# Sparse attention's row maxima without their bf16 split, a third set of split weights, the output norm's products in PSUM, and the FFN's block sums spread over the first units

## The chip, the cores and the metric

One core of one Trainium2 chip runs the whole program. The metric is the time of one execution on the device in microseconds; lower is better. Every part of the program is issued from one TileContext with `schedule_with_timeline_sim=True`: the tile scheduler, not the text, fixes the order of each engine's instructions, and each engine then runs its own list in that order, waiting on semaphores.

## The reference

One layer over 1024 tokens of width 1024: three mixers on one normalised input, merged by gates, and a gated MLP behind them. Cut to what the change touches:

```python
sc = q . kc * scale - slopes * dist_c                 # compressed branch: softmax over 63 blocks
p_cmp = masked_softmax(sc, dist_c >= 0)               # also gives the importance for top-8 selection
o_sel = masked_softmax(q . k_sel[idx] ...) @ v_sel     # selected blocks
o_win = masked_softmax(q . k_win ...) @ v_win          # window of 512
out = g0 * o_cmp + g1 * o_sel + g2 * o_win
...
mixed = gm0 * (y_ssm @ w_br_ssm) + gm1 * (y_sb @ w_br_sb) + gm2 * (y_nsa @ w_br_nsa)
x = x + rms_norm(mixed @ w_out, post_mix_norm)
h = rms_norm(x, pre_ffn_norm)
u = causal_dwconv(h @ ffn_w_up)                       # 3 taps
gate, val = split(u)
f = (gelu(gate) * val) @ ffn_w_down                   # D_FF = 2816
x = x + rms_norm(f, post_ffn_norm)
```

## The kernel before

Activations lie transposed, channels on the 128 partitions and tokens along the row, in two halves `h` of 512 tokens. Nearly every large product is made of 128x512 matmuls into a PSUM bank called `dense` (five banks) by `mm` at L203. For accuracy each fp32 operand is split into `hi` (rounded by ScalarE) and `lo` (the rest, by a subtraction), and three matmuls hi·hi, lo·hi, hi·lo stand for one product. `load_w` (L262) loads a weight block of 128x1024 (`wraw`), rounds it on ACT (L267) and subtracts on POOL (L268); it has two sets of `whi`, `wlo`, so a third unit's splits wait until PE has done with the first. A unit of one half has 24 matmuls.

**Sparse attention** runs on 16 query blocks (two groups `g`, eight blocks `i`). `compressed` (L724) makes the compressed softmax in an SBUF tile `p` and the rows that are added to the query tile `Q1`; `maxima` (L803) has PE make the scores of a block once to find each row's maximum (reduces at L826), turns the maxima into a bf16 pair (L831 to L837, five small instructions, two of POOL's memsets beside them), transposes the four 32-column pieces and copies them into `Q1[96:128]` (L842), so that the score matmuls subtract the maximum themselves. `attend` (L844) makes the scores again, exponentials and values; `merge` (L884) transposes the result, divides and adds it to `yacc` (L889 to L893). These are generators; a driver takes steps of them in turn and fills the gaps with matmuls of the merge gates' weights (`dense<-h_hi`, `h_lo`).

**Output projection and first up-units.** For each half, eight units of `wo` are followed by two norms (`rstd`, L1336 to L1340: Ln, Exp and a Newton step) and products with the norm's row (L1353, L1354, L1360); each norm's sum comes from one matmul `psn<-osq`. The result is split into `h2[h, k]`. N_FIRST = 4 pairs of up-units (`up_half`) then run plainly, all of the first half of the tokens and then all of the second, and hide the norms. The sixteen squares of `h2` are then combined (`combos`, L1428 to L1431) and split (L1500, L1501, L1506, L1507) for the other 18 pairs, which use a seven-product block scheme (`weights7`, whose weight sums are POOL's: L1391 to L1405). `conv` writes the taps of a unit (L301, L305, L309); a gate's tile then takes its Gelu (L1442) and is multiplied and stored to `m_d` (L1445, L1446).

**Down projection.** `m_chunk` loads `m_d` in chunks (L1513), splits each tile on ACT (L1519) and DVE, and `down` multiplies it with `wdn` weights of four blocks. The first chunk is asked for inside the last up-pair. The residual input `x1` (two loads of 2048 KB, L1572) is loaded early in this stage.

Of the kernel before, what the change touches and what calls it, by code (L numbers as in the profile page):

```python
# [14 lines left out]
OP = mybir.AluOpType  # L15
# [25 lines left out]
def consts():  # L41
# [24 lines left out]
    aug[0, 32:34] = 1.0  # L66
    aug[1, 34:36] = 1.0
# [127 lines left out]
def trunk(ctx: ExitStack, tc: tile.TileContext, A: dict, outT: bass.AP, dbg=None):  # L195
# [66 lines left out]
    def load_w(src, n, tiles=None, raw=None):  # L262
        if raw is None:
            raw = wp.tile([128, n], F32, name="wraw", bufs=2)
        nc.sync.dma_start(raw, src)
        hi, lo = tiles or (wp.tile([128, n], R32, name="whi", bufs=2), wp.tile([128, n], R32, name="wlo", bufs=2))
        act(hi, raw, AF.Copy)  # L267
        (V if tiles else P).tensor_tensor(lo, raw, fl(hi), op=OP.subtract)  # L268
        return hi, lo
# [28 lines left out]
    def conv(o, h, ps, taps, bias, halo, by_act=False):  # L298

        n = len(taps) - 1  # L300
        act(o, ps, AF.Identity, bias=bias, scale=taps[0])  # L301
        if h == 1 and by_act:
            for d in range(1, n + 1):
                for t in range(d):
                    act(o[:, t:t + 1], halo[:, n - d + t:n - d + t + 1], AF.Identity, bias=o[:, t:t + 1], scale=taps[d])  # L305
        if h == 0:
            V.tensor_copy(halo[:, :n], ps[:, 512 - n:])
        for d in range(1, n + 1):
            V.scalar_tensor_tensor(o[:, d:], ps[:, :512 - d], taps[d], o[:, d:], op0=OP.mult, op1=OP.add)  # L309
# [250 lines left out]
def nsa_stage(nc, tc, es, env, start):  # L560
# [162 lines left out]

    def compressed(g, i):  # L724
# [18 lines left out]
        V.tensor_tensor(pf, ps, bias, op=OP.add)  # L743
        m4 = wk.tile([128, 8], F32, name="m4")
        V.tensor_reduce(m4[:, :4], p, axis=AX, op=OP.max)
        V.tensor_tensor(p, p, m4[:, :4, None].to_broadcast([128, 4, 64]), op=OP.subtract)
        act(pf, pf, AF.Exp)
        V.tensor_reduce(m4[:, 4:8], p, axis=AX, op=OP.add)
        V.reciprocal(m4[:, 4:8], m4[:, 4:8])
        V.tensor_tensor(p, p, m4[:, 4:8, None].to_broadcast([128, 4, 64]), op=OP.mult)  # L750
# [52 lines left out]
    def maxima(g, i):  # L803
# [32 lines left out]
        V.tensor_copy(mv[:, :, :, 0], m)  # L836
        V.tensor_tensor(mv[:, :, :, 1], m, mv[:, :, :, 0], op=OP.subtract)  # L837
        yield
        p3 = ps_tb()
        for h in range(4):  # L840
            tr(p3[96:128, h * 128:(h + 1) * 128], MM[:, h, :], ident_b)
        V.tensor_copy(Q1[96:128, :], p3[96:128])  # L842

    def attend():  # L844
# [37 lines left out]
        def merge(oT, g, i, a):  # L882
# [10 lines left out]
            V.tensor_tensor(y, y, o, op=OP.add)  # L893
# [347 lines left out]
def tail_stage(nc, tc, es, env):  # L1241
# [64 lines left out]
    up_ = es.enter_context(tc.tile_pool(name="up", side="right", reuse_waits="tile", bufs=U_BUFS))  # L1306

# [4 lines left out]

    op = ExitStack()
    ow = op.enter_context(tc.tile_pool(name="ow", reuse_waits="tile", bufs=2))
    rows = []
    for h in range(2):
# [13 lines left out]
        def rstd(ss):  # L1330
# [6 lines left out]
            act(ps, ps, AF.Exp, scale=-0.5)  # L1337
# [6 lines left out]
        for j in range(8):  # L1344
            ps, = fm_unit(psd, load_w(A["wo"][j], 1024), lambda k, _: mix[h, k], 8, halves=(h,))
# [87 lines left out]
    m_d = E.scratch("m_d", [NFF * 128, T])  # L1433

    def conv(u, h, ps, st):
# [4 lines left out]
        E.conv(st[s, h], h, ps, [pvc(PV_FW, 3 * u + 2 - d) for d in range(3)], pvc(PV_FB, u), st["halo", s], True)  # L1440
        if s == 0:
            act(st[0, h], st[0, h], AF.Gelu_apprx_tanh)  # L1442
# [5 lines left out]
    def up_half(f, h, st):  # L1448
        for s in range(2):
            u = 2 * f + s  # L1450
            ps, = fm_unit(psd, load_w(A["wup"][u], 1024), lambda k, h: h2[h, k], 8, halves=(h,))
            conv(u, h, ps, st)
        gated(f, h, st)
# [30 lines left out]
    first = [{} for _ in range(N_FIRST)]  # L1484
    for h in range(2):
        for f, st in enumerate(first):
            up_half(f, h, st)

    rhs = {q: [None] * 4 for q in range(1, 8)}
    later = []  # L1490
    for k in range(4):
        quarters = [(1, h2[0, k]), (2, h2[0, k + 4]), (3, h2[1, k + 4])]
        lows = [rows[0][k], rows[1][k], rows[0][k + 4], rows[1][k + 4]]
        combos(*lows, V)
        for q, b in quarters:
            rhs[q][k] = b
        t2, t1, t4, t3 = lows
        for q, t in ((6, t2), (7, t3)):
            rhs[q][k] = hi, lo = x_t(), x_t()
            act(hi, t, AF.Copy)  # L1500
            V.tensor_tensor(lo, t, fl(hi), op=OP.subtract)  # L1501
        later += [(5, k, t1, hi_t), (4, k, t4, lo_t)]

    for q, k, t, place in sorted(later, key=lambda x: (-x[0], x[1])):
# [3 lines left out]

    acc = []

    def m_tile(f, h, s):
        t = x_t(F32) if s is None else up_.tile([128, 512], F32, name=f"u{s}")
# [3 lines left out]
    def m_split(f, h):  # L1516
        src = m_tile(f, h, None if f < DOWN[0][1] else f % 2)
# [123 lines left out]
```

## Time and profile before

| | before |
|---|---|
| median of 3 runs (lowest to highest) | 2283.76 us (2281.93 to 2283.96) |
| profiled execution | 2282.19 us, span 2280.4 us |
| mean granted TensorE clock | 0.985 |
| DVE busy | 1344.1 us (59%), 2471 instructions |
| ACT busy | 1181.0 us (52%), 2144 instructions |
| POOL busy | 1056.6 us (46%), 755 instructions |
| HBM traffic | 205.05 MB, mean 90 GB/s |

The span runs from the first to the last instruction of the profiled execution; the 1.8 us around it belong to the execution. A time in the trace is counted from the span's start. A matmul's own length (0.39 us for 128x512) is longer than the distance between two starts, since matmuls are pipelined. In a list of waits, "PE dense <- POOL wlo" is time in which PE stood still and a POOL instruction that wrote `wlo` ended last.

### The profile page before, as it was taken

The numbers are of one execution on the slowest core, as the hardware profiler recorded it, in microseconds if no ns is written. First come the engines' busy times: TensorE is split into PE (matmuls) and PEld (weight loads), VectorE is DVE, ScalarE is ACT, GpSimd is POOL, SyncE is SP. The second block draws the span as 40 slices with busy tenths as digits, with TensorE's granted clock in tenths as the row PEclk, the third lists the DMA queues.
The fourth block names the chain that finished last, engine by engine and source line by source line (L and its number), as shares of the span: only waits on it lengthen the run. The fifth ranks groups of instructions, "written<-read, shape, count | busy, mean of one in ns | idle before, by whom it ended". The sixth has DMA issues, their size and how long they took to land.

```text
span 2280.4 us, 29880 instructions
## 1 busy us (share of the span) xinstructions
PE 2187.8 (96%) x10793; PEld 1766.7 (77%) x10793; DVE 1344.1 (59%) x2471; ACT 1181.0 (52%) x2144; POOL 1056.6 (46%) x755
## 2 busy tenths in 40 slices
PE   8999998999999999999999999999889999999997
PEld 7997666667887878777777788887668888878886
DVE  8424785783367667848484543348766555643346
ACT  7144665666466676545454322245556666653124
POOL 3212565567233333444343255445588888822223
PEclk9999999999999999999999999999999999999998
DMA  5223112200111111332223363344322222263302
GB/s 194 85 83 102 51 31 70 65 13 28 64 37 52 51 47 38 109 105 70 97 75 120 118 204 113 127 146 152 107 78 83 84 83 83 97 226 112 92 29 74
DMA packets 107588, 205.05 MB, mean 90 GB/s; under 512 B 27248, under 2 KB 41392, under 8 KB 107440
## 3 DMA queue, kind: packets, MB, share of 16 engines
q1 hardware_dynamic: 107152, 202.92, 27.1%
q8 instruction: 85, 1.39, 0.3%
q14 instruction: 63, 0.52, 0.1%
q10 hardware_dynamic: 288, 0.22, 0.0%
HBM read 158.47 MB, written 44.63 MB: 89 GB/s over the span
## 4 chain that ended last, share of the span: by engine, by line
PE 75%; DVE 15%; ACT 4%; issue 3%; DMA 2%; POOL 1%; DVEq 0%; ACTq 0%; POOLq 0%
PE dense L203 60%; PE ps_s L203 5%; PE ps_o L203 4%; PE ps_t L203 4%; DVE mx L826 2%; PE ps_b L203 2%; DVE row L523 1%; POOL wlo L268 1%; DVE dec L1153 1%; DVE x L1507 1%; ACT whi L267 1%; DVE u L309 1%; DVE x L1595 0%; DMA wraw<-in_wdn 0%; DMA x<-m_d 0%
## 5 line engine op out<-in xcount | busy, mean ns | idle before, releaser
L268 POOL TENSOR_TENSOR wlo<-wraw,whi 128x1024 fp32r<-128x1024 f32 (+2 forms) x158 | 327.8, 2075 | 566.1 <-ACT whi L267 554.2
L203 PE MATMUL dense<-h_hi,whi 128*128 128x512 f32 x992 | 402.9, 406 | 8.6 <-DVE row L523 4.8
L203 PE MATMUL dense<-h_hi,wlo 128*128 128x512 f32 x992 | 390.0, 393 | 0.0
L203 PE MATMUL dense<-h_lo,whi 128*128 128x512 f32 x992 | 389.7, 393 | 0.0
L267 ACT ACTIVATE whi<-wraw 128x1024 fp32r<-128x1024 f32 (+2 forms) x158 | 141.3, 894 | 299.8 <-PE dense L203 260.8
L203 PE MATMUL dense<-hi,whi 128*128 128x512 f32 x688 | 270.9, 394 | 10.8 <-DVE u L309 5.9
L203 PE MATMUL dense<-hi,wlo 128*128 128x512 f32 x688 | 265.4, 395 | 7.9 <-POOL wlo L268 7.7
L203 PE MATMUL dense<-lo,whi 128*128 128x512 f32 x688 | 269.7, 393 | 0.1
L203 PEld LDWEIGHTS dense<-h_hi,whi 128*128 128x128 f32 x992 | 188.3, 190 | 51.6 <-issue 6.7
L203 PEld LDWEIGHTS dense<-h_hi,wlo 128*128 128x128 f32 x992 | 187.4, 189 | 40.5 <-issue 0.3
L203 PEld LDWEIGHTS dense<-h_lo,whi 128*128 128x128 f32 x992 | 188.1, 190 | 35.0 <-issue 0.4
L866 POOL TENSOR_TENSOR wT_lo<-wT,wT_hi 128x512 fp32r<-128x512 f32 x132 | 169.2, 1291 | 88.2 <-ACT wT_hi L865 80.4
L203 PEld LDWEIGHTS dense<-hi,whi 128*128 128x128 f32 x688 | 130.7, 190 | 41.1 <-ACT whi L267 7.0
L203 PEld LDWEIGHTS dense<-hi,wlo 128*128 128x128 f32 x688 | 130.6, 190 | 38.6 <-POOL wlo L268 10.4
L203 PEld LDWEIGHTS dense<-lo,whi 128*128 128x128 f32 x688 | 130.4, 190 | 28.0 <-POOL lo L1367 0.5
L203 PE MATMUL dense<-x,uhi 128*128 128x512 f32 x360 | 117.5, 391 | 4.4 <-ACT uhi L1402 3.4
L1066 POOL TENSOR_TENSOR s_lo<-sa,s_hi 128x512 fp32r<-128x512 f32 (+2 forms) x48 | 54.1, 1131 | 143.9 <-ACT s_hi L1065 133.2
L855 ACT ACTIVATE wT<-ps_s 128x512 f32<-128x512 f32 x132 | 78.4, 594 | 69.6 <-PE ps_s L203 64.9
L309 DVE SCALAR_TENSOR_TENSOR u<-dense,pv,u 128x510 f32<-128x510 f32 (+1 forms) x140 | 102.2, 742 | 10.1 <-ACT u L305 8.2
L826 DVE TENSOR_REDUCE mx<-ps_t 128x1 f32<-128x384 f32 (+3 forms) x192 | 93.9, 513 | 18.4 <-PE ps_t L203 16.3
L1535 DVE TENSOR_TENSOR x<-x,dense 128x512 f32<-128x512 f32 x64 | 43.8, 686 | 86.7 <-PE dense L203 86.6
L865 ACT ACTIVATE wT_hi<-wT 128x512 fp32r<-128x512 f32 x132 | 82.2, 629 | 13.8 <-POOL wT L857 12.1
(423 smaller groups left out, 5149.2 us busy)
## 6 DMA issues: line engine op xcount, KB each, us to landing
wraw<-in_wfm SPq DMA_DIRECT2D x62, 512.0 KB, 3.4
wraw<-in_wup SPq DMA_DIRECT2D x52, 512.0 KB, 3.3
g_d<-gate_e SPq DMA_DIRECT2D x48, 256.0 KB, 2.1
ge<-g_d SPq DMA_DIRECT2D x24, 512.0 KB, 3.8
m_d<-u SPq DMA_DIRECT2D x44, 256.0 KB, 2.0
u<-m_d SPq DMA_DIRECT2D x36, 256.0 KB, 4.3
cum<-acum_d SPq DMA_DIRECT2D x32, 256.0 KB, 3.3
wraw<-in_wo SPq DMA_DIRECT2D x16, 512.0 KB, 3.4
```

What stands on the lines that cost most here:

```text
L203: i = f(*a, **k)
L267: act(hi, raw, AF.Copy)
L268: (V if tiles else P).tensor_tensor(lo, raw, fl(hi), op=OP.subtract)
L309: V.scalar_tensor_tensor(o[:, d:], ps[:, :512 - d], taps[d], o[:, d:], op0=OP.mult, op1=OP.add)
L523: V.scalar_tensor_tensor(o[:, d:], ps[:, :512 - d], taps[d], o[:, d:], op0=OP.mult, op1=OP.add)
L826: V.tensor_reduce(mx[:, h, a, n:n + 1], pm[:, :w], axis=AX, op=OP.max)
L855: act(w.rearrange("p h q -> p (h q)"), pz, AF.Exp)
L865: act(hi, wf, AF.Copy)
L866: P.tensor_tensor(lo, wf, fl(hi), op=OP.subtract)
L1066: (P if SB_SLO else V).tensor_tensor(s_lo[:, c0:], a[:, c0:], fl(s_hi[:, c0:]), op=OP.subtract)
L1153: V.tensor_scalar(dec[:, h, :], cum[:, h, :], E.acum[:, c, 4 * q + h:4 * q + h + 1], 0.0, op0=OP.subtract, op1=OP.min)
L1535: end = V.tensor_tensor(a, a, ps, op=OP.add)
```

## The change

**Sparse attention.** Two tiles `top0`, `top1` (128 x 4 x 128, fp32) are zeroed once. For blocks with `i < 4` the reduces write straight into columns 96 and 97 of each head's square; for `i >= 4`, where a row has two parts, one more reduce does it. The scaling, the cast, the subtraction and the memsets go; the sign moves into the constant rows. The four transposes become fp32 128x128 ones, and one more step is given to the driver ahead of them. The compressed softmax and the products of `merge` stay in the PSUM bank that PE wrote.

**Output norm and first up-units.** Every third weight of the sixteen `wo` units and the first fourteen up-units gets a third set of `whi`, `wlo` (`w3`); its place is used by `weights7` afterwards. The products with the norm's row go into PSUM. The Gelus wait for the last norm's Exp that has been issued. The block sums and their splits (`columns`) are issued a step behind each unit of the second half, not after all of them.

**Down projection.** The first chunk's tiles are split while pairs 8 to 15 run (`first_split`), one in each, and both parts stored; `begin_down`, in the last pair, loads two weights and then sixteen split tiles of 256 KB straight to their places.

```diff
-    aug[0, 32:34] = 1.0
-    aug[1, 34:36] = 1.0
+    aug[0, 32] = -1.0
+    aug[1, 33] = -1.0
...
-        V.tensor_tensor(pf, ps, bias, op=OP.add)
+        V.tensor_tensor(ps, ps, bias, op=OP.add)
...
-                    V.tensor_reduce(mx[:, h, a, n:n + 1], pm[:, :w], axis=AX, op=OP.max)
+                    V.tensor_reduce(mx[:, h, a, n:n + 1] if i >= 4 else MM[:, h, 96 + a:97 + a], pm[:, :w], axis=AX, op=OP.max)
...
-        m = wk.tile([128, 4, 2], F32, name="m")
-        V.tensor_reduce(m, mx, axis=AX, op=OP.max)
-        V.tensor_scalar(m, m, -1.0, None, op0=OP.mult)
-        MM = wk.tile([128, 4, 32], BF, name="MM")
-        P.memset(MM, 0.0)
-        mv = MM[:, :, 0:4].rearrange("p h (a s) -> p h a s", a=2)
-        V.tensor_copy(mv[:, :, :, 0], m)
-        V.tensor_tensor(mv[:, :, :, 1], m, mv[:, :, :, 0], op=OP.subtract)
+        if i >= 4:
+            V.tensor_reduce(MM[:, :, 96:98], mx, axis=AX, op=OP.max)
         yield
-        p3 = ps_tb()
+        yield
+        p3 = ps_t()
         for h in range(4):
-            tr(p3[96:128, h * 128:(h + 1) * 128], MM[:, h, :], ident_b)
+            tr(p3[:, h * 128:(h + 1) * 128], MM[:, h, :], ident)
         V.tensor_copy(Q1[96:128, :], p3[96:128])
...
-            V.tensor_tensor(y, y, o, op=OP.add)
+            den, o = pbv[:, :, 64], pbv[:, :, 0:64]
+            V.reciprocal(den, den)
...
+            V.tensor_tensor(o, o, f[:, :, None].to_broadcast([128, 4, 64]), op=OP.mult)
+            V.tensor_tensor(y, o, y, op=OP.add)
...
+    def load_w3(src, n):
+        tiles = None
+        if next(count) % 3 == 2:
+            tiles = [w3.tile([128, 1024], R32, name=f"w{x}") for x in ("hi", "lo")]
+        return load_w(src, n, tiles, eng=P)
...
-            V.scalar_tensor_tensor(o[j], o[j], pvc(PV_PM, j), r, op0=OP.mult, op1=OP.mult)
-            V.tensor_tensor(o[j], o[j], x, op=OP.add)
+            p = psn.tile([128, 512], F32, name="psn", tag="psn")
+            V.scalar_tensor_tensor(p, o[j], pvc(PV_PM, j), r, op0=OP.mult, op1=OP.mult)
+            V.tensor_tensor(o[j], p, x, op=OP.add)
...
+    def first_split(f, h):
+        raw = x_t(F32)
+        nc.sync.dma_start(raw, m_d[f * 128:(f + 1) * 128, hs(h)])
+        yield
+        parts = [up_.tile([128, 512], R32, name=f"u{s}") for s in range(2)]
+        act(parts[0], raw, AF.Copy)
+        V.tensor_tensor(parts[1], raw, fl(parts[0]), op=OP.subtract)
+        for d, t in zip(ms_d, parts):
+            nc.sync.dma_start(d[f * 128:(f + 1) * 128, hs(h)], fl(t))
...
         if s == 0:
-            act(st[0, h], st[0, h], AF.Gelu_apprx_tanh)
+            with tc.issue_after(normed[0].ins):
+                act(st[0, h], st[0, h], AF.Gelu_apprx_tanh)
...
+    def columns():
+        for k in range(4):
+            blocks(k)
+            split(6, k, x_t)
+            split(7, k, x_t)
+            yield
+        for q, k, place in ((5, 0, hi_t), (5, 2, hi_t), (4, 0, lo_t), (4, 2, lo_t)):
+            split(q, k, place)
+            split(q, k + 1, place)
+            yield
...
+    for f, st in enumerate(first):
+        up_half(f, 0, st)
+    steps = columns()
+    next(steps)
+    for f, st in enumerate(first):
+        up_half(f, 1, st, lambda u: next(steps, None))
...
+    def begin_down():
+        for j in range(2):
+            ws0.append(load_w(A["wdn0"][j], DOWN[0][1] * 128))
+        ms0.update(first_chunk())
+
     for f in range(N_FIRST, NFF):
-        up_pair(f, rhs, (lambda: ms0.update(m_chunk(*DOWN[0]))) if f == NFF - 1 else None)
+        n = f - N_FIRST - 4
+        steps = first_split(n % 4, n // 4) if 0 <= n < 8 else iter(())
+        next(steps, None)
+        up_pair(f, rhs, begin_down if f == NFF - 1 else None)
+        next(steps, None)
```

What the order becomes at three places follows. **First, PE at the transposes of one block's maxima** (the sixth block, `i` = 5). `MM` and `top` are the tiles of the maxima, `Q_...` the query tiles, `ps_o` the values and `ps_s` the scores. Before:

```order
L203 MATMUL ps_o<-wT_lo,V_hi 65x512
L203 MATMUL ps_s<-Q_2716,K_1_1079 128x512
L203 MATMUL ps_s<-Q_2717,K_1_1081 128x512
L203 MATMUL ps_s<-tab,oT 128x65 x4
L203 LDWEIGHTS MM
L203 MATMUL ps_t<-ident_b,MM 32x128
```

PE at the same block in the changed kernel:

```order
L203 MATMUL ps_o<-wT_lo,V_hi 65x512
L203 MATMUL ps_s<-Q_2674,K_1_1079 128x512
L203 MATMUL ps_s<-Q_2675,K_1_1081 128x512
L203 MATMUL ps_s<-tab,oT 128x65 x4
L203 MATMUL ps_o<-wT_hi,V_hi 65x512
L203 MATMUL ps_o<-wT_hi,V_lo 65x512
L203 MATMUL ps_o<-wT_lo,V_hi 65x512
L203 MATMUL ps_t<-tab,top_1812 128x128 x4
L203 MATMUL ps_s<-Q_2929,K_0_1078 128x512
```

Three value matmuls have moved ahead of the transposes, and the first score that needs the finished `Q1` (`Q_2929`) now stands directly behind them.

**Second, PE around the last norm**, with tile numbers: `psn` is the norm's sum, `h2` of the second half is `hi_14888`, `lo_14889` before and `hi_14748`, `lo_14749` in the changed kernel. Before, at the sum:

```order
L203 MATMUL dense_15172<-lo_14483,whi_15168 128x512
L203 MATMUL psn_14879<-osq_14820,ones_66 128x512
L203 MATMUL dense_15172<-hi_14482,wlo_15169 128x512
L203 MATMUL dense_15172<-hi_14486,whi_15168 128x512
L203 MATMUL dense_15172<-lo_14487,whi_15168 128x512
```

Before, on PE, where the second half starts:

```order
L203 MATMUL dense_15210<-lo_14517,whi_15206 128x512
L203 MATMUL dense_15210<-hi_14516,wlo_15207 128x512
L203 MATMUL dense_15249<-hi_14888,whi_15245 128x512
L203 MATMUL dense_15249<-lo_14889,whi_15245 128x512
L203 MATMUL dense_15249<-hi_14888,wlo_15246 128x512
```

PE in the changed kernel, at the sum:

```order
L203 MATMUL dense_15069<-hi_14343,wlo_15064 128x512
L203 MATMUL psn_14739<-osq_14673,ones_66 128x512
L203 MATMUL dense_15069<-hi_14348,whi_15063 128x512
L203 MATMUL dense_15069<-lo_14349,whi_15063 128x512
L203 MATMUL dense_15069<-hi_14348,wlo_15064 128x512
```

And PE in the changed kernel, where the second half starts:

```order
L203 MATMUL dense_15069<-lo_14369,whi_15063 128x512
L203 MATMUL dense_15069<-hi_14368,wlo_15064 128x512
L203 MATMUL dense_15120<-hi_14748,whi_15116 128x512
L203 MATMUL dense_15171<-hi_14748,whi_15167 128x512
L203 MATMUL dense_15223<-hi_14748,whi_15217 128x512
L203 MATMUL dense_15120<-lo_14749,whi_15116 128x512
```

Between the sum and the first use of the second half's `h2` stood 46 matmuls; now there are 15, and three units start together where one did.

**Third, the end of the up-pairs.** ACT's list in the last two pairs before (`hi<-x` is the split of the first chunk's tiles, `uhi` a rounded weight sum, `u`, `snap` the taps):

```order
L1399 ACTIVATE uhi<-uf_18302 128x1024
L1423 ACTIVATE snap<-dense 128x512 x2
L1519 ACTIVATE hi<-x 128x512 x2
L267 ACTIVATE whi<-wraw 128x512
L1404 ACTIVATE ahi<-wraw 128x512
L1519 ACTIVATE hi<-x 128x512
L301 ACTIVATE u_18255<-dense,pv 128x512
L301 ACTIVATE u_18274<-snap,pv 128x512
L1519 ACTIVATE hi<-x 128x512
L305 ACTIVATE u_18274<-halo,u_18274,pv 128x1 x2
L1402 ACTIVATE uhi<-uf_18301 128x1024
```

ACT's list there in the changed kernel:

```order
L1407 ACTIVATE uhi<-uf_18232 128x1024
L1431 ACTIVATE snap<-dense 128x512 x2
L1412 ACTIVATE ahi<-wraw 128x512
L267 ACTIVATE whi<-wraw 128x512
L301 ACTIVATE u_18185<-dense,pv 128x512
L301 ACTIVATE u_18204<-snap,pv 128x512
L305 ACTIVATE u_18204<-halo,u_18204,pv 128x1 x3
L1410 ACTIVATE uhi<-uf_18231 128x1024
```

The splits that waited for loads of `m_d` no longer stand among the others. They, their loads and their stores lie in earlier pairs; SP's list in two middle pairs before:

```order
L1446 DMA m_d<-u_16632 128x512
L1446 DMA m_d<-u_16721 128x512
L1385 DMA wraw<-in_wup 128x1024 x2
L1446 DMA m_d<-u_16788 128x512
L1446 DMA m_d<-u_16877 128x512
```

And SP's list in the changed kernel, in one of pairs 8 to 15:

```order
L1393 DMA wraw<-in_wup 128x1024 x2
L1476 DMA m_d<-u_16352 128x512
L1452 DMA mhi_d<-u_16451 128x512
L1452 DMA mlo_d<-u_16452 128x512
L1446 DMA x<-m_d 128x512
L1476 DMA m_d<-u_16441 128x512
L1393 DMA wraw<-in_wup 128x1024 x2
```

Two stores and a load stand now between the loads of one pair's weights and the next's.

More of the change, by code (lines that the diff above doesn't have):

```diff
@@ L722, in nsa_stage @@
     wk = es.enter_context(tc.tile_pool(name="nsa_q", reuse_waits="tile", bufs=2))
+    tops = [wk.tile([128, 4, 128], F32, name=f"top{n}", bufs=1) for n in range(2)]
+    for t in tops:
+        P.memset(t, 0.0)
     def compressed(g, i):
@@ L1315, in tail_stage @@
     rows = []
+    normed = [None]
     for h in range(2):
@@ L1433, in tail_stage, with first_chunk @@
     m_d = E.scratch("m_d", [NFF * 128, T])
+    ms_d = [E.scratch(f"m{x}_d", [DOWN[0][1] * 128, T]) for x in ("hi", "lo")]
+    def first_split(f, h):
[7 more added lines that the diff above has]
+            nc.sync.dma_start(d[f * 128:(f + 1) * 128, hs(h)], fl(t))
+    def first_chunk():
+        ms = {}
+        for h in range(2):
+            for f in range(DOWN[0][1]):
+                ms[f, h] = hi_t(), lo_t()
+                for d, t in zip(ms_d, ms[f, h]):
+                    nc.sync.dma_start(fl(t), d[f * 128:(f + 1) * 128, hs(h)])
+        return ms
     def conv(u, h, ps, st):
@@ L1439, in conv @@
         st[s, h] = up_.tile([128, 512], F32, name=f"u{s}")
-        E.conv(st[s, h], h, ps, [pvc(PV_FW, 3 * u + 2 - d) for d in range(3)], pvc(PV_FB, u), st["halo", s], True)
+        end = E.conv(st[s, h], h, ps, [pvc(PV_FW, 3 * u + 2 - d) for d in range(3)], pvc(PV_FB, u), st["halo", s], True)
         if s == 0:
-            act(st[0, h], st[0, h], AF.Gelu_apprx_tanh)
+            with tc.issue_after(normed[0].ins):
+                act(st[0, h], st[0, h], AF.Gelu_apprx_tanh)
+        return end
     def gated(f, h, st):
@@ L1446, in gated, with up_half @@
         nc.sync.dma_start(m_d[f * 128:(f + 1) * 128, hs(h)], st[0, h])
-    def up_half(f, h, st):
+    def up_half(f, h, st, then=None):
         for s in range(2):
             u = 2 * f + s
-            ps, = fm_unit(psd, load_w(A["wup"][u], 1024), lambda k, h: h2[h, k], 8, halves=(h,))
-            conv(u, h, ps, st)
-        gated(f, h, st)
+            ps, = fm_unit(psd, (load_w3 if 2 * f + s + 8 * h < 14 else load_w)(A["wup"][u], 1024),
+                          lambda k, h: h2[h, k], 8, halves=(h,))
+            end = conv(u, h, ps, st)
+            if s == 1:
+                gated(f, h, st)
+            if then:
+                with tc.issue_after(end.ins):
+                    then(u)
     def up_pair(f, rhs, between=None):
@@ L1481, in up_pair, with blocks, split @@
         gated(f, 1, st)
[L1484 to L1487, printed above, removed]
     rhs = {q: [None] * 4 for q in range(1, 8)}
-    later = []
-    for k in range(4):
-        quarters = [(1, h2[0, k]), (2, h2[0, k + 4]), (3, h2[1, k + 4])]
+    sums = {}
+    def blocks(k):
         lows = [rows[0][k], rows[1][k], rows[0][k + 4], rows[1][k + 4]]
         combos(*lows, V)
-        for q, b in quarters:
+        for q, b in ((1, h2[0, k]), (2, h2[0, k + 4]), (3, h2[1, k + 4])):
             rhs[q][k] = b
         t2, t1, t4, t3 = lows
[L1498 to L1504, printed above, removed]
+        sums.update({(6, k): t2, (7, k): t3, (5, k): t1, (4, k): t4})
+    def split(q, k, place):
+        t = sums[q, k]
         rhs[q][k] = hi, lo = place(), x_t()
@@ L1507, in tail_stage @@
         V.tensor_tensor(lo, t, fl(hi), op=OP.subtract)
+    def columns():
[8 more added lines that the diff above has]
+            yield
+    first = [{} for _ in range(N_FIRST)]
+    for f, st in enumerate(first):
[4 more added lines that the diff above has]
+        up_half(f, 1, st, lambda u: next(steps, None))
+    w3_.close()
+    wx_ = ExitStack()
+    wx = wx_.enter_context(tc.tile_pool(name="wx", reuse_waits="tile", bufs=2))
+    fw = es.enter_context(tc.tile_pool(name="ffn", side="right", reuse_waits="tile", bufs=1))
     acc = []
     def m_tile(f, h, s):
-        t = x_t(F32) if s is None else up_.tile([128, 512], F32, name=f"u{s}")
+        t = up_.tile([128, 512], F32, name=f"u{s}")
         nc.sync.dma_start(t, m_d[f * 128:(f + 1) * 128, hs(h)])
```

50 lines of the change are left out of this document (25 added, 25 removed).

## The prediction

> **What bounds the kernel now.** I began with the page's busy times and its chain of waits.
>
> ```profile
> PE 2187.8 (96%) x10793; PEld 1766.7 (77%) x10793; DVE 1344.1 (59%) x2471; ACT 1181.0 (52%) x2144; POOL 1056.6 (46%) x755
> PE 75%; DVE 15%; ACT 4%; issue 3%; DMA 2%; POOL 1%; DVEq 0%; ACTq 0%; POOLq 0%
> ```
>
> PE is busy for 96% of the span and the chain runs through it for 75%. So at most 2280.4 - 2187.8 = 92.6 us of idle PE can go, and besides that what half-speed stretches cost; the change removes hardly any PE work. The second view is therefore what PE waited for (engine, line, releaser: us in total, times, longest us).
>
> ```profile
> PE ps_t L203 <- DVE MM L837: 10.1, 8, 2.5
> PE dense L203 <- POOL wlo L268: 7.7, 5, 5.4
> PE dense L203 <- DVE u L309: 5.9, 1, 5.9
> PE dense L203 <- ACT whi L267: 4.9, 5, 1.9
> PE dense L203 <- ACT uhi L1402: 3.4, 2, 3.2
> ```
>
> These five rows, 32.0 us, all lie where the change works: MM at the maxima, the others around the norm, the first pair and the last pair. The third view, stretches of 60 us with each engine's busy time, shows how much is lost there.
>
> ```profile
> 1560.00:1620.00 60.00, 55.24 (x230) 42.50 (x230) 54.05 (x84) 37.31 (x51) 29.39 (x15) 1.00 0.42 141
> 1620.00:1680.00 60.00, 47.35 (x191) 37.70 (x191) 44.68 (x46) 32.14 (x61) 39.01 (x17) 0.89 0.29 97
> 1680.00:1740.00 60.00, 60.00 (x266) 49.65 (x265) 34.78 (x42) 35.45 (x62) 48.88 (x29) 1.00 0.22 75
> 1980.00:2040.00 60.00, 55.18 (x236) 44.91 (x234) 35.53 (x44) 34.63 (x65) 24.04 (x14) 0.97 0.55 189
> ```
>
> The third row is a stretch without a loss: 266 matmuls in 60 us, 0.2256 us from start to start. Against it the first two rows miss 36 and 75 matmuls, 8.1 and 16.9 us; the last misses 30, 6.8 us. The loss is more than the idle time because the granted clock falls too (PE's own windows: busy, clock, DMA share, GB/s):
>
> ```profile
> 1672.00:1676.00 4.00, 0.00 (x0) 0.59 0.29 95
> 1676.00:1680.00 4.00, 4.00 (x10) 0.56 0.27 101
> ```
>
> After a stall of 6 us, 10 matmuls ran in 4 us where 17.7 fit: 7.7 x 0.2256 = **1.7 us more for each long stall**. I use that price for every stall that goes or comes with over 3 us.
>
> **A, sparse attention: -7 us.** The worst wait is after the maxima of one block:
>
> ```profile
> 378.74 1.18 DVE L836 CAST MM<-m 128x8 bf16<-128x8 f32 x1
> 379.95 2.26 DVE L837 TENSOR_TENSOR MM<-m,MM 128x8 bf16<-128x8 f32 x1
> 382.27 0.44 PE L203 MATMUL ps_t<-ident_b,MM 128*32 128x128 bf16 x4 [2.51 <-DVE MM L837]
> ```
>
> Eight elements a lane cost 3.4 us there. These instructions go; what stays ahead of the transposes is the last reduce, and for `i >= 4` one more small one. Of the 10.1 us of these waits I leave 1.2 (order changes, some covers are still short): -8.9; half a clock price more, at 382.3, goes: -0.9. The transposes grow:
>
> ```profile
> 253.61 0.40 PE L203 MATMUL ps_t<-ident_b,MM 128*32 128x128 bf16 x4
> 254.69 0.60 PE L203 MATMUL ps_b<-tab,qd 128*128 128x128 f32 x4
> ```
>
> Four of the new kind (the second row has their shape) take 0.20 us more than four of the old; 16 blocks, +3.2. By the Trainium skill, "TensorE: Matmul & The Clock Gate", Part 4, a full 128x128 transpose took about 275 ns in one kernel's context; were that their pace, A would end above zero instead of at -7. The second row disagrees: four in 0.60 us are 0.11 apart, and I price by it. New waits come where a score stands directly behind the transposes and needs `Q1` from a DVE copy: two blocks had that before, four have it now, two more at 0.8, +1.6 (an estimate from these waits' own length). Products kept in PSUM shorten DVE:
>
> ```profile
> L893 DVE TENSOR_TENSOR yacc<-yacc,ob 128x256 f32<-128x256 f32 x29 | 19.4, 669 | 0.3
> ```
>
> Both inputs in SBUF take 669 ns. With one in PSUM I take about 0.42, the length of the product just before it in the same chain, an estimate: 29 x 0.25 = 7 us of DVE, off the path mostly; I count 2 of it for PE's other small waits there. Sum -8.9 - 0.9 + 3.2 + 1.6 - 2 = **-7**, between -11 (no new waits, all 10.1 gone) and -2 (a wait of 0.8 at eight blocks more).
>
> From the end of attention to 1500 us only the scheduler's placing changes: 0, with 3 us either way.
>
> **B, norm and first units: -9 us.** What is lost before comes from two long stalls.
>
> ```profile
> 1617.72 7.66 POOL wlo L268
> 1625.42 0.80 PE L203 MATMUL dense<-hi,wlo 128*128 128x512 f32 x1 [5.39 <-POOL wlo L268]
> 1665.02 9.01 DVE L1507 TENSOR_TENSOR x<-x,lo 128x512 fp32r<-128x512 f32 x4
> 1676.00 0.80 PE L203 MATMUL dense<-hi,whi 128*128 128x512 f32 x1 [5.89 <-DVE u L309]
> ```
>
> The first: a `wlo` of 7.66 us, beside a row of block sums on DVE, just when its weight had to wait for a free set. With a third set it can be made a unit earlier, and the sums come a few at a time: 5.4 + 1.7 and about 1.4 of the `whi` waits beside it go, 1 us stays: -7.5. The second: four subtractions of 2.25 us on DVE, beside POOL's weight sums, stand ahead of the eighth unit's conv, which has to give its bank back. In the new order these four stand there again, and a subtraction of the first pair with them. But between the first pair's start and the bank it needs now stand 60 matmuls, not 40: 20 x 0.2256 = 4.5 us of cover more. Of 5.9 us 1.4 are left, too short for the clock: -6.2. Some small waits of the same stretch: -1.3.
>
> Against it stands the last norm. Its chain from sum to `h2` in rows (the table load and a Gelu on ACT; products, a Newton step and the first products with the row on DVE; a `lo` on POOL):
>
> ```profile
> 1593.97 1.28 ACT L1336 ACT_TABLE_LOAD   x1
> 1595.27 0.66 ACT L1336 ACTIVATE psn<-psn,eps 128x512 f32<-128x512 f32 x1
> 1609.96 0.63 ACT L1442 ACTIVATE u<-u 128x512 f32<-128x512 f32 x1
> 1598.46 0.68 DVE L1445 TENSOR_TENSOR u<-u,u 128x512 f32<-128x512 f32 x1
> 1599.07 0.68 DVE L1339 SCALAR_TENSOR_TENSOR osq<-osq,psn 128x512 f32<-128x512 f32 x1
> 1600.51 2.72 DVE L1360 SCALAR_TENSOR_TENSOR x<-x,pv,psn 128x512 f32<-128x512 f32 x4
> 1609.98 1.74 POOL L1367 TENSOR_TENSOR lo<-x,hi 128x512 fp32r<-128x512 f32 x1
> ```
>
> In the new order Ln and Exp need no load ahead of them (2 x 0.66), but then come a load and the held Gelus (1.28 + 0.63), and DVE has three gate products between the Newton steps, each behind its Gelu: 1.3 + 1.9 + six DVE instructions of 0.68 (4.1) = 7.3 to the finished row, then a conv that is queued ahead (0.8), the first product (0.7) and its `hi` (0.6): about 9.4 us. PE has 15 matmuls to do meanwhile, 3.4 us, where before it had 46, 10.4. So a **new stall of 6.0 us** at the second half's start, with 1.7 for the clock; before, some 1.7 us were lost there in short waits, which go: +6. Sum -7.5 - 6.2 - 1.3 + 6 = **-9**. Bounds: -14, if DVE takes the chain without the gate products' wait (5 us less); -2, if both long stalls keep half of their length.
>
> **C, end of the up-pairs and first chunk: -8.5 us.**
>
> ```profile
> 2001.76 0.63 ACT L1519 ACTIVATE hi<-x 128x512 fp32r<-128x512 f32 x1 [0.80 <-DMA x<-m_d]
> 2002.85 1.04 ACT L1402 ACTIVATE uhi<-uf 128x1024 fp32r<-128x1024 f32 x1
> 2003.94 1.22 PE L203 MATMUL dense<-x,uhi 128*128 128x512 f32 x2 [3.22 <-ACT uhi L1402]
> 2040.29 0.50 PE L203 MATMUL dense<-hi,whi 128*128 128x512 f32 x1 [1.89 <-ACT whi L267]
> 2029.70 0.57 SPq L265 DMA_DIRECT2D wraw<-in_wdn  x1
> 2036.00:2040.00 4.00, 2.40 (x11) 1.00 1.06 403
> ```
>
> ACT waited for a load of `m_d` with the weight sum queued behind it; those splits are elsewhere now: -3.2 - 1.7. The second wait is for a down weight issued at 2029.70, into a stretch where the DMA share is 1.06 and 403 GB/s move, while `x1` loads. Five weights instead of four are issued ahead of `x1` in the new order: -1.9 - 1.7. What is added: 16 tiles of 256 KB, 4.2 MB, loaded in place of half as much, 10 us at that rate, with the last pair's 19 us and two units' 11 us as cover, and no wait by my margin of 6 us. Without that cover the same 10 us less 6, some 4, would stand on PE. The splits in the pairs cost ACT 0.63 and DVE 0.68 each, beside PE work of 19 us a pair. Sum **-8.5**, between -9 and -3 (the second wait stays, a short one at the tiles comes).
>
> **Sum:** 2282.2 (the profiled execution) - 7 - 9 - 8.5 = 2257.7. The median of the runs is 1.6 us above that execution: **2259 us**.
>
> **Rivals.**
> 1. *The norm's stall is longer.* Where the products beside POOL run at the 2.25 us of the 1665.02 row and not 0.68, five of them add 8 us to the chain, and B gives nothing. 2259 + 8 = 2267. For it: POOL makes every `lo` of the norm and of the weights there. Against: four of the chain's products have an input in PSUM.
> 2. *The port stays the bound.* Splits and sums keep both inputs in SBUF, and POOL's `wlo` runs beside them; the third set moves the meeting, it doesn't end it. Then the 1669 stall stays (+6.2) and half of the 1619 one (+4): 2269. The Trainium skill, "SBUF — State Buffer", Who interferes with whom, says it as a rule: a DVE instruction with two SBUF inputs contends with a GpSimd instruction that reads SBUF, and `tensor_reduce` never does. The 9.01 and 7.66 us rows agree with the first half.
> 3. *Slower: SP's queue in pairs 8 to 15.* Two stores that wait for ACT and DVE stand there ahead of weight loads:
>
> ```profile
> 1808.90 8.46 SPq L1446 DMA_DIRECT2D m_d<-u  x2
> 1819.54 6.39 SPq L1385 DMA_DIRECT2D wraw<-in_wup  x2
> ```
>
> The last store was through at 1817.4 and the loads at 1819.5, so 2.2 us of lateness cost nothing. Beyond that each us is PE's, eight times, and POOL, 48.88 of 60 us busy there, can't catch up. At 5.2 us late each pair loses 3.0 + 1.7 = 4.7: 2259 + 38 = 2297. It turns the result from a loss of 3.6 a pair on, 4.1 us late. Against: the stores fall between two `m_d` stores that are 8 us apart, and PE lost nothing in that stretch.
> 4. *It doesn't do what it says.* A's blocks wait for `Q1` instead (0), the norm's stall eats B (0), C gives 3: 2281.
>
> **How the numbers follow.** Forecast 0.52, rivals 0.15, 0.15, 0.10, 0.08. The range takes in A, B and C at odds with each other (one at its good end, -12 from 2259; for the other side rivals 1 and 2 with a bound of 8 more): 2247 to 2277; outside are rivals 3 and 4 and a little. A measurement here tells about 0.2%, 4.6 us. Faster by more: 0.52 + 0.15 + 0.15 = 0.82; within: 0.08; slower: 0.10.
>
> **What would show it.** Right: no PE wait on a DVE maximum over 1 us between 228 and 540; no PE idle of 5 us on `wlo` near the second half; a new one of about 6 us there on the rounded `h2`; 266 matmuls per 60 us through pairs 8 to 15; no wait on `uhi` in the last pair. Wrong: waits on DVE's `Q1` copy at more than four blocks, a conv wait near the first pair that keeps 5 us, or PE waits that repeat every 19 us between 1750 and 1910.

## The result, and the profile after

| | before | changed |
|---|---|---|
| median (lowest to highest), 4 runs each | 2282.85 us (2280.33 to 2283.96) | 2252.27 us (2251.32 to 2252.72) |
| ratio, 95% interval | | 0.9867 (0.985 to 0.9884) |
| span of the profiled execution | 2280.4 us | 2249.6 us |
| mean granted TensorE clock | 0.985 | 0.989 |

The change takes 30.6 us away, 24.8 were forecast; 2252.27 lies in the range of 2247 to 2277. The page of the changed kernel, busy times and chain by engine:

```profile
PE 2172.8 (97%) x10793; PEld 1763.4 (78%) x10793; DVE 1305.5 (58%) x2415; ACT 1176.7 (52%) x2141; POOL 1049.9 (47%) x725
PE 85%; DVE 8%; ACT 3%; issue 2%; DMA 1%; POOL 1%; DVEq 0%; SPq 0%; ACTq 0%; POOLq 0%
```

PE has the same 10793 matmuls; its share of the chain went from 75% to 85%, DVE's from 15 to 8. Idle PE fell from 92.6 us to 2249.6 - 2172.8 = 76.8. Its waits that bear on the changed stages (total, times, longest; larger ones, such as 7.4 us on ACT's `thi`, 6.7 on `psn` and 6.3 on `row`, belong to other stages):

```profile
PE dense L203 <- ACT hi L1374: 6.1, 1, 6.1
PE dense L203 <- POOL wlo L1399: 4.8, 1, 4.8
PE ps_s L203 <- DVE Q L843: 4.1, 4, 1.3
PE dense L203 <- DVE u L309: 3.3, 3, 1.1
PE ps_t L203 <- DVE top L832: 0.9, 3, 0.4
```

None of the five rows of before is left as it was, and three of these are new: a rounded `h2` tile, a `lo` of the first pair's weights, and three conv waits. To see what each stage gave, I summed from each trace, matmul by matmul, how much later the next one started than the usual distance for its kind; that counts idle time and half-clock stretches alike. The columns hang on the usual distance that one takes; the differences between them do so less:

| stage, between events on PE | lost before, us | lost after, us |
|---|---|---|
| start to the first transposes of `Q1` | 15.0 | 12.8 |
| to the last transposes of maxima | 55.7 | 38.3 |
| to the last gate matmul | 78.7 | 80.7 |
| to the first norm sum | 3.0 | 2.5 |
| to the last norm sum | 5.6 | 1.4 |
| to the first rounded weight sum (first pair) | 13.2 | 16.4 |
| the next quarter of the pairs | 8.5 | 0.4 |
| the other pairs | 5.0 | 4.2 |
| 100 us behind them | 4.1 | 0.0 |
| to the end | 8.3 | 8.4 |
| all | 197.1 | 165.1 |

32.0 us less, minus 1.7 us more of matmul work (the larger transposes, at the usual distance taken for them), is 30.3; the spans differ by 30.8.

In windows around the norm and in the pairs, PE's busy time, clock, DMA share and GB/s of the changed kernel:

```profile
1560.00:1620.00 60.00, 53.89 (x226) 0.94 0.40 130
1620.00:1680.00 60.00, 55.06 (x233) 0.94 0.26 85
1680.00:1740.00 60.00, 60.00 (x267) 1.00 0.26 88
1800.00:1860.00 60.00, 58.88 (x260) 1.00 0.36 119
1980.00:2040.00 60.00, 60.00 (x266) 1.00 0.73 250
```

The row of 1980 has lost nothing, where 30 matmuls were missing; the first two still miss 40 and 33; and pairs 8 to 15, without loss before, miss 6 in 60 us. The forecast new stall, in the timelines of DVE and ACT (start, duration, instruction, and in brackets the idle time before it and its releaser), with PE's row last:

```profile
1581.50 0.69 DVE L1348 TENSOR_TENSOR osq<-osq,psn 128x512 f32<-128x512 f32 x1 [1.34 <-ACT psn L1347]
1583.44 0.69 DVE L1475 TENSOR_TENSOR u<-u,u 128x512 f32<-128x512 f32 x1 [1.25 <-ACT u L1471]
1584.05 0.68 DVE L1349 SCALAR_TENSOR_TENSOR osq<-osq,psn 128x512 f32<-128x512 f32 x1
1584.65 1.28 DVE L1475 TENSOR_TENSOR u<-u,u 128x512 f32<-128x512 f32 x2
1585.86 0.69 DVE L1350 SCALAR_TENSOR_TENSOR psn<-osq,psn 128x512 f32<-128x512 f32 x1
1588.12 2.60 ACT L1374 ACTIVATE hi<-x 128x512 fp32r<-128x512 f32 x4 [1.54 <-DVE x L1371]
1588.80 1.65 PE L203 MATMUL dense<-hi,whi 128*128 128x512 f32 x3 [6.11 <-ACT hi L1374]
```

Between two Newton steps DVE waits 1.25 us for a Gelu and does a gate product, then two more; the row is finished at 1586.6, 7.9 us after the sum's matmul started at 1578.7, and PE, whose 15 matmuls behind the sum lasted 4.0 us, waits 6.11. From the first of these 15 to the first use of `h2` it is 10.1 us.

### The profile page after: what moved, and what is told of

Read it like the earlier page. It is cut to its first block, busy times and chain, and to the rows that moved or that the text cites. A ratio compares the mean times of both kernels' runs of the same rounds, so it can differ in the third digit from the quotient of the medians.

```text
span 2249.6 us, 29858 instructions
## 1 busy us (share of the span) xinstructions
PE 2172.8 (97%) x10793; PEld 1763.4 (78%) x10793; DVE 1305.5 (58%) x2415; ACT 1176.7 (52%) x2141; POOL 1049.9 (47%) x725
## 4 chain that ended last, share of the span: by engine, by line
PE 85%; DVE 8%; ACT 3%; issue 2%; DMA 1%; POOL 1%; DVEq 0%; SPq 0%; ACTq 0%; POOLq 0%
PE dense L203 67%; PE ps_s L203 6%; PE ps_o L203 5%; PE ps_t L203 4%; PE ps_b L203 2%; DVE u L309 1%; DVE mx L832 1%; DMA cum<-acum_d 1%; DVE x L1656 0%; DVE x L1534 0%; ACT h_hi L395 0%; ACT wT L856 0%; DVE dec L1154 0%; DVE row L524 0%; DVE row L1219 0%
## 5 line engine op out<-in xcount | busy, mean ns | idle before, releaser
L268 POOL TENSOR_TENSOR wlo<-wraw,whi 128x1024 fp32r<-128x1024 f32 (+2 forms) x158 | 320.7, 2030 | 568.7 <-ACT whi L267 544.0
L203 PE MATMUL ps_s<-Q,K 128*128 128x512 f32 x264 | 83.6, 398 | 4.2 <-DVE Q L843 4.1
```

The costliest lines, as they stand in the source:

```text
L203: i = f(*a, **k)
L268: (eng or (V if tiles else P)).tensor_tensor(lo, raw, fl(hi), op=OP.subtract)
```

## Experiments

Each run is compared with runs of the kernel before on the same chip; those medians lay between 2277.6 and 2281.9 us, single runs between 2274 and 2286. Verdicts below rest on the waits in each trace at least as much as on these times.

**1. Sparse attention's edits alone**, on the kernel before (`aug`, `tops`, `compressed`, `maxima`, `merge` of the change, nothing else).

> The kernel before with only the sparse attention's edits (maxima, compressed softmax and merge in PSUM). Theory 1, from the two traces: between the first transposes of Q1 and the last maxima PE lost 55.7 us to waits and half-speed stretches before and 38.4 with the whole change, so 17.3 less; the bigger transposes take back 2.3 and the stretch behind loses 2.0 more. Expected 2283 - 13 = 2270 us (2268 to 2272), with no wait on MM left, four waits on the Q1 copy of 4.1 us in all, and the clock at 1.00 from 360 to 480 us, where it was 0.97. Theory 2, the size in my prediction (-7): the rest of the 17 comes from elsewhere, 2276 us.

2265.66 us against 2278.71, ratio 0.9938 (0.9923 to 0.9953): -13.1. The stage lost 38.4 us, as in the changed kernel; no wait on a maximum's small instructions, no window under a clock of 0.97 there, four `Q1` waits of 4.1. Theory 1 holds: the edits are worth 13 us, about twice what I forecast.

**2. The maxima alone**, the softmax and `merge` staying in SBUF.

```diff
-        m = wk.tile([128, 4, 2], F32, name="m")
...
+        if i >= 4:
+            V.tensor_reduce(MM[:, :, 96:98], mx, axis=AX, op=OP.max)
```

> The kernel before with only the maxima's edits; the compressed softmax and merge stay in SBUF. Theory 1: the maxima carry the waits on MM (10.1) and the two half-speed stretches behind them (3.4), less 2.3 for transposes and 2.5 for new waits on Q1: -9, 2274 us; the missing 4 us to the run with all attention edits are DVE time that the products in PSUM set free. Theory 2: the products in PSUM are hidden anyway, and this run equals that one, 2270 us.

2276.22 us against 2278.71, ratio 0.9988 (0.9978 to 0.9998): -2.5, neither theory's number. The stage lost 48.0 us: 7.7 less than before and 9.6 more than with all three edits. So **the products in PSUM carry more than half of the stage's gain**, on top of the maxima's edits; they were not run without these, nor the softmax apart from `merge`. DVE's groups over the stage, by shape (total, mean ns, idle before), first with the maxima alone, then with all attention edits:

```profile
L892 DVE TENSOR_TENSOR yacc<-yacc,ob 128x256 f32<-128x256 f32 x28 | 18.3, 652 | 0.3
L889 DVE TENSOR_TENSOR of<-of,sg 128x4 f32<-128x4 f32 x29 | 14.0, 482 | 0.7
L750 DVE TENSOR_TENSOR cp<-cp,m 128x256 f32<-128x256 f32 x13 | 10.7, 822 | 0.3
```

```profile
L893 DVE TENSOR_TENSOR yacc<-ps_s,yacc 128x256 f32<-128x256 f32 x28 | 11.6, 416 | 0.3
L891 DVE TENSOR_TENSOR of<-ps_s,sg 128x4 f32<-128x4 f32 x29 | 4.6, 160 | 1.0 <-DVE ps_s L890 0.4
L751 DVE TENSOR_TENSOR ps_b<-ps_b,m 128x256 f32<-128x256 f32 x13 | 5.6, 431 | 0.4
```

The same work takes 43.0 us in the first set of rows and 21.8 in the second. Even four elements a lane cost 482 ns with both inputs in SBUF and 160 with one in PSUM. That agrees with the Trainium skill, "SBUF — State Buffer", Who interferes with whom: an instruction with two SBUF inputs contends with a GpSimd instruction that reads SBUF, and one with a single SBUF input, outside its two-port modes, does not. DVE's reduces of scores stand in the same queue, and the bank that PE waits for is freed behind them: the waits on `mx`, `top`, `oT` and `Q1` are 9.9 us with the maxima alone, and 6.3 with all edits; a half-clock stretch at 300 us, which only the former has, costs some 1.7 more, and the rest is in delays of under 0.3 us.

**3. The first down chunk alone**, on the kernel before (`first_split`, `first_chunk`, `begin_down`).

> The kernel before with only the first down chunk's edits (split early, stored, loaded straight into place). Theory 1: the stalls of 3.2 and 1.9 us with their clock, 9.1 us together, go, and three conv waits of 1.1 us come in pairs 8 to 15, with about 1 us of short ones: -5, 2278 us. Theory 2: the waits of the pairs belong to the changed stages ahead, not to the chunk: none here, -9, 2274 us.

2277.55 us against 2278.71, ratio 0.9991 (0.9981 to 1.0001): -1.2. The interval includes no change at all, so the times alone show no gain; the waits do. The waits of PE in the pairs and behind them, in this run and, for comparison, in the trace of before:

```profile
PE dense L203 <- DVE u L309: 3.3, 3, 1.1
```

```profile
PE dense L203 <- ACT uhi L1402: 3.2, 1, 3.2
PE dense L203 <- ACT whi L267: 1.9, 1, 1.9
```

Both old waits are gone and three conv waits have come, with nothing else changed: theory 2 falls. The size is less sure than the mechanism: in experiments 1 and 2, where this part is unchanged, the old two waits are 1.2 and 2.1, and 2.5 and 3.2 us, and the loss from there to 100 us behind the pairs 5.9 and 9.8, against 4.2 here. So this part gives 1.7 to 5.6 us by trace. What one of the three convs waits for, on DVE in the changed kernel:

```profile
1782.63 2.91 DVE L1475 TENSOR_TENSOR u<-u,u 128x512 f32<-128x512 f32 x1
1785.47 1.78 DVE L309 SCALAR_TENSOR_TENSOR u<-snap,pv,u 128x510 f32<-128x510 f32 x1
1787.17 1.78 DVE L1450 TENSOR_TENSOR u<-x,u 128x512 fp32r<-128x512 f32 x1
1788.87 0.15 DVE L307 COPY halo<-dense 128x2 f32<-128x2 f32 x1
1788.94 2.96 DVE L309 SCALAR_TENSOR_TENSOR u<-dense,pv,u 128x511 f32<-128x511 f32 x4
```

The chunk's own subtraction (L1450), 1.78 us, stands ahead of the conv that gives PE its bank back. It isn't the whole cause: it took 1.77 to 1.78 us in all eight pairs of units there, and PE waited in three of them, every second one, 39.5 us apart. In those three the gate product ahead of it (L1475) took 2.91 us, as shown, against 0.68 or 0.69 before the next subtractions, and from its start to that of the subtraction it is 4.5 us instead of 3.4. Why in every second one is open.

**4. The Gelus held behind `h2`'s fourth tile**, on the changed kernel.

```diff
-            normed[0] = act(ps, ps, AF.Exp, scale=-0.5)
+            act(ps, ps, AF.Exp, scale=-0.5)
...
-                act(hi, o[j], AF.Copy)
+                a = act(hi, o[j], AF.Copy)
+                if j == 3:
+                    normed[0] = a
```

> The changed kernel with the Gelus of the first half held behind the fourth rounded tile of the second half's h2 instead of behind the last norm's Exp; PE's order around the norm is the same, 15 matmuls of cover. Theory 1: the stall of 6.1 us at the second half's start is the norm's chain, in which DVE waits 1.25 us for a Gelu and spends 1.9 on three gate products between the Newton steps: the stall falls to 3.0 us, 2249 us if its half clock stays, 2247.5 if not. Theory 2: the stall is set by the conv queued ahead of the first product, which waits for PE's last unit: it stays near 6 us, 2252 us.

2255.5 us, ratio 0.9895 (0.988 to 0.9909). PE's waits from 1480 to 1760 us:

```profile
PE dense L203 <- DVE u L309: 4.0, 1, 4.0
PE dense L203 <- ACT whi L1400: 3.2, 1, 3.2
PE dense L203 <- ACT hi L1374: 2.4, 1, 2.4
PE dense L203 <- POOL lo L1380: 1.3, 1, 1.3
PE dense L203 <- POOL wlo L1401: 0.4, 1, 0.4
```

Theory 1 was right on the stall: 2.4 us with a second wait of 1.3 behind it, instead of 6.1. It was wrong on the time: 3.6 us on the weights of the first pair and 4.0 on the eighth unit's conv, the very wait that the change had removed, make up for it. Something behind PE sets when this stretch ends.

**5. The Gelus not held at all** (`issue_after` taken out).

> The changed kernel with the Gelus free to run as soon as their tiles are ready. Two table loads come back ahead of the last norm's Ln and Exp (2 x 1.28), two of the three gate products leave its chain, and the scheduler puts the norm's sum 9 matmuls nearer to the second half (6 matmuls of cover instead of 15, 2.0 us less). Theory 1: the chain is about as long as with the hold and the stall grows by the cover lost, from 6.1 to about 7.5 us: 2253 to 2255 us. Theory 2: the held Gelus are what makes the chain long, and without them the stall is under 4 us: 2249 us.

2256.36 us, ratio 0.9891 (0.9867 to 0.9914); the stall is 8.2 us and the wait on the first pair's `wlo` 6.8. Theory 1 holds: from the first matmul behind the sum to the first use of `h2` it is 10.2 us without the hold and 10.1 with it, so the chain isn't shorter, and the sum stands nearer.

**6. Two sets of split weights** (`if next(count) % 3 == 2` to `if False`).

> The changed kernel with two sets of split weights again. Theory 1: the third set took away the waits on whi and wlo at the start of the second half (7.5 us with their clock by my prediction) and brought the norm's stall, since PE gets to the second half sooner: with two sets 46 matmuls of cover stand behind the norm's sum again, the stall of 6.1 us falls to nothing, and waits on whi and wlo of 5 us or more come back; the sum is near zero, 2250 to 2255 us. Theory 2: the third set is a gain by itself, 2258 to 2261 us.

2254.87 us, ratio 0.9884 (0.9865 to 0.9904): theory 1. The rounded `h2` is no wait any more; a `lo` of it (1.8), `whi` and `wlo` of the units (1.9 and 1.4), the first pair's `wlo` (2.7) and the conv (2.6) are. The third set moved the wait, and gained some 2 us at most.

**7. All block sums behind the last unit**, as before the change.

```diff
-        up_half(f, 1, st, lambda u: next(steps, None))
+        up_half(f, 1, st)
+    for _ in columns():
+        pass
```

> The changed kernel with all block sums and their splits issued behind the last unit of the second half, as before the change. Theory 1: spreading them is what took away the stall on the eighth unit's conv; with them at the end, DVE and ACT do some 32 instructions of 0.7 us or more while the first pair waits for them, so 5 to 10 us come back between the second half and the first pair: 2257 to 2262 us. Theory 2: the third set already parts the sums from the weights' splits, and the place of the sums doesn't matter: 2252 us.

2253.88 us, ratio 0.9881 (0.9861 to 0.99): theory 2. The stall stays at 6.1, the first pair's `wlo` takes 2.3 and a unit's `wlo` 1.8; spreading the sums is worth next to nothing.

**8. The first pair's `lo` ahead of the weight sums** on POOL.

```diff
+        if turn[0] == 2:
+            with tc.issue_after(made.ins):
+                P.tensor_tensor(u1, a21, a22, op=OP.add)
```

> The changed kernel with the first pair's lo part of its first weights made by POOL ahead of the weight sums, not behind five of them. Theory 1: the wait of 4.8 us on it and the half clock behind it (1.7) go, and the weight sums, 2.4 us later, are still in time, since PE needs the first of them 7 us later: 2246 us. Theory 2: the loss moves to the next thing that is late there (the eighth unit's conv, behind DVE's subtractions, or the rounded weight sums): 2250 to 2253 us.

2257.01 us, ratio 0.9895 (0.9875 to 0.9916). Theory 2: the wait on `wlo` fell from 4.8 to 0.6 us, and the conv's, which the change had brought to nothing, is 7.0. The `h2` stall stays at 6.1, and a wait of 2.0 on a unit's `uhi` is new.

```profile
PE dense L203 <- DVE u L309: 7.0, 1, 7.0
PE dense L203 <- POOL wlo L1399: 0.6, 1, 0.6
```

**9. Three repairs together**: experiments 4 and 8, and the first half's last unit ordered behind the norm's sum on PE.

```diff
+            with tc.issue_after(summed[0].ins) if (f, h, s) == (N_FIRST - 1, 0, 1) else ExitStack():
+                ps, = fm_unit(psd, w, lambda k, h: h2[h, k], 8, halves=(h,))
```

> The changed kernel with three repairs: the last unit of the first half behind the norm's sum on PE (24 matmuls of cover), the Gelus held behind the fourth tile of h2, the first pair's first lo ahead of the weight sums. Theory 1 (each stall is its own, and what is removed is gained): no stall over 1.5 us before the first pair, 18.2 us of loss between the norm's sum and the fourth pair fall to 8: 2242 us. Theory 2 (DVE's splits ahead of the eighth unit's conv bound this stretch, and whatever is gained ahead of them is waited for there): the conv's wait grows to 7 us or more, as it did with the lo alone (7.0), and the time stays at 2251 to 2256 us.

2254.63 us, ratio 0.988 (0.9862 to 0.9897). Theory 2, in PE's two longest waits and in DVE's timeline:

```profile
PE dense L203 <- DVE u L309: 7.0, 1, 7.0
PE dense L203 <- ACT hi L1374: 2.2, 1, 2.2
```

```profile
1639.55 4.50 DVE L1541 TENSOR_TENSOR x<-x,hi 128x512 fp32r<-128x512 f32 x2
1643.97 10.11 DVE L1541 TENSOR_TENSOR x<-x,lo 128x512 fp32r<-128x512 f32 x4
1654.01 0.74 DVE L309 SCALAR_TENSOR_TENSOR u<-dense,pv,u 128x511 f32<-128x511 f32 x1
```

Six subtractions, 2.2 to 2.5 us each beside POOL's weight sums, stand ahead of the eighth conv. PE's other waits are a `uhi` and a `lo` of 2.0 each and a `wlo` of 0.4. What PE saves ahead of the conv, it spends waiting for it.

**10. The same, and the last four of these subtractions behind that conv.**

```diff
-        up_half(f, 1, st, lambda u: next(steps, None))
+        up_half(f, 1, st, lambda u: [next(steps, None) for _ in range({5: 0, 6: 0, 7: 2}.get(u, 1))])
```

> The same three repairs, and the last four splits (the operands of product 4) issued behind the eighth unit's conv: two subtractions stand ahead of it on DVE instead of six. Theory 2: the conv's wait is these subtractions, 2.3 to 2.8 us each beside POOL, so it falls by 7 us or more to under 1, and PE waits for product 4's operands by no more than 3: 2243 to 2246 us. Theory 3: POOL's weight sums, not DVE's order, bound the first pair, and the wait appears on a weight sum or its rounding instead: 2251 to 2256 us.

2246.58 us, ratio 0.9838 (0.9813 to 0.9863). The conv is 10.5 us earlier on DVE than in experiment 9, and of PE's waits from 1480 to 1760 us are left:

```profile
PE dense L203 <- ACT hi L1374: 2.2, 1, 2.2
PE dense L203 <- POOL lo L1380: 2.0, 1, 2.0
PE dense L203 <- ACT uhi L1416: 2.0, 1, 2.0
PE dense L203 <- POOL wlo L1401: 0.2, 1, 0.2
```

```profile
1643.50 0.74 DVE L309 SCALAR_TENSOR_TENSOR u<-dense,pv,u 128x511 f32<-128x511 f32 x1
1645.42 3.75 DVE L1541 TENSOR_TENSOR x<-x,lo 128x512 fp32r<-128x512 f32 x2
1652.63 2.75 DVE L1541 TENSOR_TENSOR x<-x,lo 128x512 fp32r<-128x512 f32 x2
```

Theory 2 is confirmed: with the three repairs in place, putting four instructions elsewhere is worth 8 us. That move on the change alone was not run, so how the gain divides between it and the three repairs is open. Theory 3 falls; no weight sum took the wait over, and the `uhi` wait of 2.0 was there in experiment 9 too.

**11 and 12. That kernel once more, and the changed kernel beside it** on one chip.

> The kernel of the run before (three repairs and the last four splits behind the eighth conv) once more, beside the changed kernel on the same chip. If the loss between the norm's sum and the fourth pair is 12.5 us against 16.8 (the sums of PE's losses there in the two traces), it is 4 to 6 us faster than the changed kernel.

> The changed kernel itself, for the comparison on one chip: within 3 us of 2252 us, and 4 to 6 us slower than the run beside it.

2246.49 us (2245.01 to 2247.94) and 2253.40 us (2251.81 to 2253.98); ratios to before 0.9861 (0.984 to 0.9883) and 0.9891 (0.9873 to 0.9909). The two sets of runs don't overlap: the version of experiment 10 beats both kernels, the changed one by 6.9 us, a little more than the 4 to 6 expected. Among experiments 4 to 9, which lie within 3.1 us of each other on different chips, the times don't settle an order; their traces do the telling.

## Why the prediction was right, and where it was not

**Direction and place were right**: the time went where PE waited, in the three stages named, and the order of the chain's links stands.

**A was mis-sized, -7 against -15** (17.4 lost less, 1 to 2 of larger transposes; the 13 of experiment 1 have the 2.0 in them that are lost behind it). By its own terms: the waits on MM went wholly (-10.1 for -8.9); the transposes were priced too high, +3.2 for some +1.2: from a block's first transpose to the next matmul it is 0.36 us against 0.33 where nothing waits, and 0.20 more only in the four blocks with a wait; the new waits on `Q1` are four blocks, as read from the order, and 2.5 us more than before, for +1.6. The clock gave 3.4 us, not 0.9: there were two half-speed stretches, at 382 and 464 us, and I counted half of one. But the step that failed is "I count 2 of it for PE's other small waits there": keeping the products in PSUM was sized at 2 us, and experiments 1 and 2 put 9.6 us of PE's losses on it. The duration was right (0.42 us estimated, 416 ns measured); what I took for "off the path mostly" was the queue in which PE's banks are freed.

**The middle**, 0 with 3 either way: +2.0. It came with the attention edits, as experiment 1 has it too: PE's waits on `row` behind the attention rose from 4.8 to 6.3 us, and one of 1.0 on `state` is new.

**B was right in its main term, and with some luck in its sum, -9.1 lost less against -9.** The new stall was forecast at 6.0 us and measured 6.11, though the chain took 10.1 us, not 9.4, and the cover was 4.0, not 3.4: two errors that cancel. The first long stall went, as forecast. The second was to keep 1.4 us of its wait; it went from the conv, but a wait of 4.8 us on the first pair's `lo` stands in its place; with the slow clock behind it, it costs some 7 us that the sum didn't have, and about as much more went than was counted. B also hangs on the one trace of before: with the conv's wait of experiments 2 and 3 (2.5 us, not 5.9) it would be some 4 us smaller. And the reasons given for the gains were not all causes: the third set alone (experiment 6) and the spread sums (7) are worth little by themselves. In experiments 4, 8 and 9 what was saved ahead of the eighth conv was waited for there. That is rival 2, with another price than it had: the conv's subtractions beside POOL bound the stretch, as experiments 8 to 10 show, though they show as no wait at all in the changed kernel's trace, where the four of them are no faster and PE just comes as late:

```profile
1643.94 9.08 DVE L1534 TENSOR_TENSOR x<-x,lo 128x512 fp32r<-128x512 f32 x4
```

**C was too large, -4.9 lost less against -8.5.** Both waits went as forecast, and the sixteen loads cost PE nothing; but "the splits in the pairs cost ACT 0.63 and DVE 0.68 each, beside PE work" was wrong: the subtraction took 1.78 us and stood ahead of a conv that PE waited for three times, 1.1 us each and some 0.5 us in slower starts. That is about the 3.6 us that C lacks. Experiment 3 shows them without the other edits.

**The other rivals.** Rival 1, a longer norm chain, didn't come: the products took 0.64 to 0.69 us each. Those that read PSUM did so beside POOL's work; the gate products between them have both inputs in SBUF and were as fast, with POOL idle from 1579.7 to 1586.0. Rival 3 didn't come either: no wait repeats every 19 us, and PE's only waits between 1760 and 2080 us are the three conv waits, 39.5 us apart. Rival 4 is out. Of the signs, the one for pairs 8 to 15, 266 matmuls in 60 us, failed (260 or 261), and the first pair's `wlo` wait of 4.8 us came near the 5 that spoke against.

The difference was larger than the forecast by 5.8 us: A gave 8 more, C 3.6 less, the middle 2.0 less, and 2.2 us less were lost ahead of the attention, in a part that the change doesn't touch (12.8 to 15.0 us in the traces, whatever the kernel). That makes 4.6; the norm's sum, with 0.5, and the rounding and scatter of the runs and their medians make up the rest.

## What to carry to other kernels

An instruction off the path is not free when it stands in the queue that hands back PE's banks: ask of each small instruction what is queued behind it, and keep one operand in PSUM where POOL reads SBUF meanwhile. Where two engines end a stretch together, removing the wait that shows can move it to the one that doesn't; look one link on in the other engine's list, and repair both or neither. A cover is counted in PE's order from the releasing event on, and can shrink because PE got faster.

## What was not expected of the hardware

The granted clock fell behind a wait of 2.5 us: at 382 us in the kernel before, two windows of 4 us show 0.81 and 0.76. In experiment 2 it fell to 0.79 and 0.78 behind one of 1.9 us, at 300 us. Waits of up to 1.3 us left it above 0.96 in experiment 1, but in the kernel before two waits of 1.1 and 0.8 us close together at 462 us came ahead of a window at 0.57, and a like pair at 280 us left it at 1.00. So no threshold is shown. The kernel before, then experiment 2:

```profile
380.00:384.00 4.00, 1.73 (x11) 0.81 0.00 0
384.00:388.00 4.00, 4.00 (x20) 0.76 0.64 210
```

```profile
300.00:304.00 4.00, 2.08 (x9) 0.79 0.00 0
304.00:308.00 4.00, 4.00 (x19) 0.78 0.12 35
```

The same order of instructions doesn't stall alike in each kernel: the eighth conv's wait was 5.9 us in the trace of before and 2.5 in experiments 2 and 3, whose code and order there are the same. What set it was not tried; the kernel before scatters over 2274 to 2286 us, the changed one over 2251 to 2254.
